# Two lag matrices at the end of the scan's program instead of among the late state products

## The chip, the cores and the metric

The kernel runs on one core of one Trainium2 chip. The metric is the device time of one execution in microseconds; the kernel before takes 1023.78 us (median of three runs, 1023.33 to 1025.45).

## The reference, cut to what matters

One layer of a diffusion backbone over 1024 latent tokens and 256 context tokens, of width 1024: a bidirectional state-space mixer (S5: 64 groups of 16 channels with 64 complex states each, a scan forward and one backward), a GELU and a gated linear unit, then a feed-forward block (SwiGLU, hidden width 2816), with adaptive norms around both.

```python
def s5_direction(u_ctx, u_lat, ...):
    lam_bar = exp(lam * exp(log_step))
    b_bar = ((lam_bar - 1) / lam) * b
    def run(u, h0):
        bu = einsum('lgh,gnh->lgn', u, b_bar);  bu[0] += lam_bar * h0
        h = associative_scan(h[l] = lam_bar * h[l-1] + bu[l])
        return einsum('lgn,ghn->lgh', h, c).real, h[-1]
    y_c, h_c = run(u_ctx, 0)
    y_l, _ = run(u_lat, h_c)
    return y_c, y_l
...
g = gelu(y_forward + y_backward + d_skip * h)
x = x + gate * (g * sigmoid(g @ w_glu + b_glu))
x = x + gate2 * swiglu(modulate(rms_norm(x)))
return rms_norm(x, norm_final)
```

## The kernel before, in words

The sequence is cut into 160 chunks of 8 tokens (32 of context, 128 of latents). Inside a chunk the outputs that come from the chunk's own inputs are a product with a lag matrix (a Toeplitz matrix made of c, the powers of lam_bar and b_bar, for each group); what comes from earlier chunks is a product of c times powers with the state at the chunk's start. The states themselves come from a serial scan over the chunks on VectorE (`scan()`, line 77 with LTa, LTb and ltc in PSUM), which runs while the other engines prepare what they can.

The 64 groups are held in four quarters of 16, and each quarter in two halves of 8; so there are eight halves, k = 0 to 7. Quarters 0 to 2 (k = 0 to 5) get their output in two steps: an early one that needs only the first half of the scan, and a late one for the second half of the latents. The last quarter (k = 6 and 7) gets all of it in one step at the end.

The order of the work around the change is written by hand as two strings of letters, PROG1 and PROG2; `run(prog)` goes through them and calls a function for each. Each engine works through its own instructions in that order. The scan's instructions are issued to VectorE ahead of both, so PROG1 is what the other engines do meanwhile. The letters that matter:

- C: the factors of c and powers of a quarter, on GpSimd (the last of them C33; the last quarter's lie in the region c3).
- K: `k_mats`, the lag matrices of one half. 144 small matmuls on TensorE (lines 809, 813 and 817; each with its weight load) write two PSUM banks, of which only some rows are written, so the banks are zeroed first. ScalarE copies each bank to SBUF (line 821) and issues a write of it to a table in HBM (line 822, tensor kd). K0 to K5 are in PROG1, zeroed by ScalarE (line 771) or standing in banks that keep their zeros (kt and pm). K6 and K7 are in PROG2; their banks are zeroed there by VectorE memsets (letters k6 and k7, line 966).
- T: `toeplitz`, SP reads a shifted quarter of a table back into SBUF (line 830). T12 to T15 belong to the last quarter.
- P and Y: the early product of a half (lines 945 and 922) and its two copies out of PSUM on ScalarE (line 997). P5 is the last.
- M2, m0, F30, F31: small products on GpSimd and a read by SP; F fills in the states between those that the scan has made, for the last quarter.
- Z, N, D, H: the late step of k: a turned copy of the states (Z, on VectorE or ScalarE, lines 902 and 904), the product (N, 64 matmuls, line 922), the addition on VectorE (D) and the GELU on ScalarE (H).
- Q: the whole product of a half of the last quarter (lines 945 and 935); it reads what T has brought.
- I and J: transposes of the activations for the GLU (line 1056) and their split in two parts for precise products; w and l: SP's reads of GLU weights (lines 1024 and 1048); W and V: the weights' split by VectorE, ScalarE and GpSimd; g: the first GLU products.

After PROG1 the PSUM pools of that stage are closed and eight banks (tile pe) opened in their place; a bank of the new pool is free when the last reader of the old one is done.

Of the kernel before, what the change touches and what calls it, by code (L numbers as in the profile page):

```python
# [25 lines left out]
HC = 16  # L26
# [2 lines left out]
MAGIC = 12582912.0  # L29
HOWS = "PPPP PPEE PEEE EEEE"  # L30
ZEN = "VVSVSVSV"
PROG1 = ("A22 B0 A26 C02 G1 A30 A34 C03 A40 K0 A44 A48 C10 K1 L2 A54 G2 C11 A60 F10 C12 F11 C13 T0 T1 T2 T3 A64 M0 M1 K2 R0 P0 Y0 Y1 K3 L3 R1 C20 P1 Y2 Y3 T4 T5 G3 T6 T7 C21 C22 C23 K4 R2 P2 Y4 Y5 K5 R3 P3 Y6 Y7 T8 T9 T10 T11 C30 C31 R4 P4 Y8 Y9 C32 C33 R5 P5 Y10 Y11 M2 m0 F30 F31")
PROG2 = ("k6 Z0 N0 Z1 Z2 D0 Z3 N1 k7 D1 Z4 H0 H1 K6 N2 D2 H2 K7 T12 T13 T14 T15 N3 Z5 D3 H3 N4 D4 z6 z7 I0 J0 I1 J1 w0 w1 l1 H4 N5 D5 I2 J2 H5 I3 J3 W0 W1 x0 x1 x2 x3"
         " Q6 H6 I4 J4 Q7 b0 I5 J5 H7 g03 g13 I6 J6 g23 g05 g15 I7 J7 V1 w20 w21 g26 x10 x11 x12 x13")
LOG2E = 1.4426950408889634
LN2H = 0.693359375
# [6 lines left out]
def s5_ffn_kernel(tc, a, out):  # L43
    nc = tc.nc
    V, S, E, PE, SY = nc.vector, nc.scalar, nc.gpsimd, nc.tensor, nc.sync
    ctx = ExitStack()
    with ctx:
        ctx.enter_context(tc.manual_schedule())
        sb = ctx.enter_context(tc.tile_pool(name="sb", bufs=1))
        def region(tag, kb, dt=F32):  # L50
            return sb.tile([P, int(kb * 256)], dt, tag=tag, name=tag)
# [12 lines left out]
        R0 = region("r0", 7)  # L64
# [79 lines left out]
        def pw(shape=(4, P)):  # L144
            return pW.tile([P] + list(shape), F32, tag="w", name="pw", bufs=NW[0])
# [613 lines left out]
        pm = pW.tile([P, 512], F32, tag="m", name="pm")  # L759
# [10 lines left out]
        def zeros(t):  # L770
            S.copy(t, cpk[:, 0:1].to_broadcast([P, 15 * HC]))
            return t

        kt = zeros(pA.tile([P, 15 * HC], F32, tag="r3", name="kt"))
# [24 lines left out]
        def bb(q, d, ri, a_):  # L799
            return BBn[q // 2][:, ri, d, 8 * (q % 2) + a_]  # L800

        def k_mats(q, hq, kts):

            tiles = [(g_, 2 * gi + hq, kts[g_][32 * gi:32 * gi + HC], slice(64 * g_, 64 * g_ + 64), (64 * g_, 32 * gi))
                     for gi in range(4) for g_ in range(2)]
            for d, c0, c1, ts_ in ((1, 128, 240, slice(7, 0, -1)), (0, 0, 112, slice(6, None, -1))):
                for ri in range(2):
                    for g_, a_, kv, ps, tp in tiles:
                        PE.matmul(kv[:, c0:c1], bb(q, d, ri, a_)[ps], CL[q][ps, ri, d, a_, ts_], start=ri == 0, stop=ri == 1,
                                  tile_position=tp)  # L810
            for g_, a_, kv, ps, tp in tiles:
                l0 = 64 * g_ + HC * (tp[1] // 32)
                PE.matmul(kv[:, 112:128], ident[ps, l0:l0 + HC], KD[ps, q, hq], start=True, stop=False, tile_position=tp)
            for d in range(2):
                for ri in range(2):
                    for g_, a_, kv, ps, tp in tiles:
                        PE.matmul(kv[:, 112:128], bb(q, d, ri, a_)[ps], Cs[q % 2][ps, 0, ri, d, a_], start=False,
                                  stop=d + ri == 2, tile_position=tp)
            for g_ in range(2):
                gq, kx = 2 * hq + g_, KX[2 * hq + g_]  # L820
                S.copy(kx, kts[g_])
                S.dma_start(KD_[q][:, gq], kx)
# [52 lines left out]
        def mod_cols(part):  # L875
            r8 = view(RA, 0, [4, P])
            if part == 0:
                S.copy(r8, pm.rearrange("p (j n) -> p j n", j=4))
                for i in range(2):
                    SY.dma_start(MBd[i], r8[96 * i:96 * i + 2].rearrange("p j n -> p (j n)"))  # L880
            elif part == 1:
                pt = pw()
                for j in range(4):
                    PE.transpose(pt[:, j], r8[:, j], ident)
                for h in range(2):
                    S.copy(mcol[:, :, 4 * h:4 * h + 4].rearrange("p b j -> p j b"), pt[:, :, h:P:32])
            elif part == 2:
                E.tensor_copy(mod2[:, 0], mcol[:, 1])
                tt(mod2[:, 1], mcol[:, 2], epsc[:, 1:2].to_broadcast([P, T]), ADD, E)
                tt(mod2[:, 1], mod2[:, 1], nrm[:, 1], MUL, E)  # L890
# [63 lines left out]
        def run(prog):  # L954


            for w in prog.split():
                op, i = w[0], int(w[1:])
                if op == "A":
                    ada(i)  # L960
                elif op == "M":
                    mod_cols(i)
                elif op == "k":
                    KT[i] = [pe8([15 * HC]) for _ in range(2)]
                    for kv in KT[i]:
                        V.memset(kv, 0.0)
                elif op == "K":
                    k_mats(*divmod(i, 2), KT.get(i) or [kt, zeros(pw([15 * HC])) if i < 4 else pm[:, 0:15 * HC]])
                elif op == "L":
                    cs_load(i, S)  # L970
                elif op == "G":
# [66 lines left out]
                elif op == "g":  # L1038
                    glu_mm(0, i // 10, range(i % 10 + 1))

        KT = {}
        late, W0, WR, PZ, GH, GR = {}, [], [], {}, [None, None], []
        wr0 = [view(RXa, 4, [1024]), view(RW, 0, [1024])]
        bglu = view(RU, 32, [D])
# [5 lines left out]
        def pe8(shape, tag="e", bufs=8):  # L1050
            return pE.tile([P] + list(shape), F32, tag=tag, name="pe", bufs=bufs)
# [51 lines left out]

        HOW = [[{"P": PE, "Y": SY, "E": E, "V": V}[c] for c in h] for h in HOWS.split()]
        run(PROG1)
        psW.__exit__(None, None, None)
        psA.__exit__(None, None, None)
        psE = tc.tile_pool(name="psE", bufs=1, space=bass.MemoryType.PSUM, reuse_waits="tile")
        pE = psE.__enter__()
        run(PROG2)  # L1110
        W0, GR = W0[0], GR[0]
        X1 = region("c3", 16)
# [92 lines left out]
        for cq in range(4):  # L1205
            for s in range(4):
                k = 4 * cq + s
# [61 lines left out]
        G2 = region("c3", 16, R32)  # L1269
# [420 lines left out]
        for i, (kind, ft, j) in enumerate(seq):  # L1690
# [12 lines left out]
            if kind == "U":  # L1703
# [4 lines left out]
                if (ft, j) in LAST:  # L1708
                    k, h = LAST[ft, j]
# [63 lines left out]
```

## Time and profile before

| | us |
|---|---|
| median of three runs | 1023.78 (1023.33 to 1025.45) |
| profiled execution, span | 1022.5 |
| TensorE busy | 962.6 (94%) |
| VectorE busy | 785.6 (77%) |
| GpSimd busy | 762.7 (75%) |
| ScalarE busy | 438.5 (43%) |

The profile gives the execution's own time only as its span, from the first instruction to the last; the runs' time is taken around it. In what follows a row of a timeline has the start, the duration, the engine, the line and the operation with the tiles that it writes and reads, and in brackets the idle time before it with what ended it. PEld is TensorE's weight load, which overlaps its matmuls; SPq and ACTq are transfers issued by SyncE and ScalarE. Tile names have no buffer numbers.

### The profile page before, as it was taken

The page shows a single profiled execution, that of the slowest core. Times are in us where ns is not written, and L with a number is a line of the kernel's source. Part 1 is how long each engine was busy: PE and PEld are TensorE (multiplying, and loading weights), DVE is VectorE, ACT ScalarE, POOL GpSimd, SP SyncE. Part 2 cuts the span into 40 slices and gives each one's busy share as a digit, 9 for nine tenths or more (in the row PEclk, how much of TensorE's full clock was granted, in tenths as well). Part 3 has the DMA queues.
Part 4 walks back from the last instruction along what each step waited for, and adds up shares of the span by engine and source line. Part 5 has one row for each costly group of instructions (what it writes and reads, how often), then busy time and mean ns, then how long its engine had stood idle before and what let it go on. Part 6 is the DMA issues. An engine that isn't in the chain of part 4 may idle for free. (4 is left out here: it accounts for less than half of the span.)

```text
span 1022.5 us, 18552 instructions
## 1 busy us (share of the span) xinstructions
PE 962.6 (94%) x6988; PEld 774.2 (76%) x6988; DVE 785.6 (77%) x1642; ACT 438.5 (43%) x858; POOL 762.7 (75%) x590
## 2 busy tenths in 40 slices
PE   5987798868999999999999999999999999999996
PEld 1466523658999988778888888888888888888885
DVE  7989799994365778788968768585958778686977
ACT  5477622324353663533334343424333343324337
POOL 5799999991591457879686877778686877777664
PEclk9999999998999999999999999999999999999998
DMA  9765997222622021011212011121212111121205
GB/s 318 292 132 96 276 350 243 91 73 57 235 80 86 2 104 62 21 42 42 83 41 73 32 52 61 43 73 52 73 42 81 41 40 56 45 70 52 72 21 165
DMA packets 48546, 98.96 MB, mean 97 GB/s; under 512 B 4284, under 2 KB 18876, under 8 KB 47176
## 3 DMA queue, kind: packets, MB, share of 16 engines
q1 hardware_dynamic: 43272, 86.64, 25.3%
q0 software_dynamic: 2016, 7.34, 3.8%
q10 hardware_dynamic: 3168, 3.79, 1.1%
q8 instruction: 55, 0.90, 0.4%
q14 instruction: 35, 0.29, 0.1%
HBM read 84.25 MB, written 6.17 MB: 88 GB/s over the span
## 5 line engine op out<-in xcount | busy, mean ns | idle before, releaser
L77 POOL TENSOR_TENSOR c<-rxc,c 128x512 fp32r<-128x512 f32 x128 | 166.6, 1316 | 53.5 <-ACT c L1227 52.7
L1287 PE MATMUL ut<-ra,c 128*128 128x512 f32 x400 | 155.7, 389 | 1.2 <-DVE ra L77 1.2
L1286 PE MATMUL ut<-ra,c 128*128 128x512 f32 x400 | 155.7, 389 | 0.2 <-ACT ra L1227 0.2
L1288 PE MATMUL ut<-ra,c 128*128 128x512 f32 x400 | 155.6, 389 | 0.0
L1227 ACT CAST c<-rxc 128x512 fp32r<-128x512 f32 x128 | 79.1, 622 | 146.8 <-PE xt L1581 53.3
L1581 PE MATMUL xt<-c,c 128*128 128x512 f32 x540 | 129.7, 389 | 0.0
L1581 PEld LDWEIGHTS xt<-c,c 128*128 128x128 f32 x540 | 101.4, 188 | 21.0
L77 DVE TENSOR_TENSOR ru<-ru,xt 128x1024 f32<-128x1024 f32 x90 | 106.8, 1213 | 8.6 <-PE xt L1581 6.6
L77 DVE TENSOR_TENSOR ru<-ut,ru 128x512 f32<-128x512 f32 x98 | 67.1, 686 | 43.1 <-PE ut L1288 37.7
L1287 PEld LDWEIGHTS ut<-ra,c 128*128 128x128 f32 x400 | 75.1, 188 | 17.1 <-POOL rxc L77 1.5
L1286 PEld LDWEIGHTS ut<-ra,c 128*128 128x128 f32 x400 | 75.1, 188 | 16.1 <-ACT ra L1227 0.6
L1288 PEld LDWEIGHTS ut<-ra,c 128*128 128x128 f32 x400 | 75.1, 188 | 15.5
L77 POOL TENSOR_TENSOR c<-rw,c 128x512 fp32r<-128x512 f32 (+1 forms) x29 | 42.5, 1465 | 38.8 <-ACT c L1227 38.2
L1286 PE MATMUL ut<-c,c 128*128 128x512 f32 x160 | 62.3, 389 | 0.8 <-DVE rxa L77 0.8
L77 POOL TENSOR_TENSOR c<-ru,c 128x512 fp32r<-128x512 f32 (+1 forms) x39 | 55.5, 1422 | 10.1 <-ACT c L1227 5.7
L77 POOL TENSOR_TENSOR rxc<-rxc 128x512 f32<-128x512 f32 x40 | 61.5, 1536 | 1.6
L1288 PE MATMUL ut<-c,c 128*128 128x512 f32 x160 | 62.3, 389 | 0.0
L1287 PE MATMUL ut<-c,c 128*128 128x512 f32 x160 | 62.3, 389 | 0.0
L1581 PE MATMUL ut<-c,c 128*128 128x512 f32 x216 | 51.9, 389 | 0.0
L584 PE MATMUL pv<-ru,c 128*64 128x160 f32 x512 | 43.7, 312 | 7.3 <-POOL ru L77 2.6
L77 DVE TENSOR_TENSOR pe<-pe,ru 128x256 f32<-128x256 f32 x64 | 27.4, 428 | 29.5 <-ACT pe L1127 17.4
L77 DVE TENSOR_TENSOR ru<-ru,ut 128x512 f32<-128x512 f32 x76 | 47.2, 678 | 0.7 <-ACT ru L1635 0.5
(449 smaller groups left out, 2576.0 us busy)
## 6 DMA issues: line engine op xcount, KB each, us to landing
c<-in_ada_w SPq DMA_DIRECT2D x46, 256.0 KB
rxc<-in_w SPq DMA_DIRECT2D x38, 256.0 KB
rxc<-in_w SPq DMA_DIRECT2D x19, 512.0 KB
ru<-in_w SPq DMA_DIRECT2D x11, 512.0 KB
rw<-in_w SPq DMA_DIRECT2D x11, 512.0 KB
ra<-in_ada_w SPq DMA_DIRECT2D x10, 512.0 KB
ra<-in_ada_w SPq DMA_DIRECT2D x18, 256.0 KB
ru<-in_xT SPq DMA_DIRECT2D x4, 1024.0 KB
```

Of the source, the lines that this page charges most:

```text
L77: eng.tensor_tensor(out=o, in0=x, in1=y, op=op)
L584: PE.matmul(pv[64 * (i % 2):64 * (i % 2) + 64, ri, c0:c0 + 160], w[:, i, 64 * ri:64 * ri + 64], U[:, 8 * b + 4 * j + i], start=True, stop= ...
L1227: S.copy(o[0], x)
L1286: PE.matmul(pu, wh, bh, start=start, stop=False)
L1287: PE.matmul(pu, wh, bl, start=False, stop=False)
L1288: PE.matmul(pu, wl, bh, start=False, stop=stop)
L1581: PE.matmul(pd, w[:, cs_], b, start=j in (1, 2, 4) and n == 0, stop=n == 2, skip_group_check=j not in (1, 2, 4))
```

## The change

K6 and K7 move from PROG2 to PROG1, behind the copies of the last early product (Y10, Y11) and ahead of M2, K7 first. K7 uses the banks kt and pm as K5 does, with no new zeros; K6 gets two banks of the pool pw, zeroed by ScalarE. The four VectorE memsets go. T12 to T15 stand first in PROG2 now, and the reads w0, w1 and l1 of the GLU weights stand after H2 and ahead of N3, no longer behind J1.

```diff
-PROG1 = ("... R5 P5 Y10 Y11 M2 m0 F30 F31")
-PROG2 = ("k6 Z0 N0 Z1 Z2 D0 Z3 N1 k7 D1 Z4 H0 H1 K6 N2 D2 H2 K7 T12 T13 T14 T15 N3 Z5 D3 H3 N4 D4 z6 z7 I0 J0 I1 J1 w0 w1 l1 H4 N5 D5 I2 J2 H5 I3 J3 W0 W1 x0 x1 x2 x3"
+PROG1 = ("... R5 P5 Y10 Y11 K7 K6 M2 m0 F30 F31")
+PROG2 = ("T12 T13 T14 T15 Z0 N0 Z1 Z2 D0 Z3 N1 D1 Z4 H0 H1 N2 D2 H2 w0 w1 l1 N3 Z5 D3 H3 N4 D4 z6 z7 I0 J0 I1 J1 H4 N5 D5 I2 J2 H5 I3 J3 W0 W1 x0 x1 x2 x3"
          " Q6 H6 I4 J4 Q7 b0 I5 J5 H7 g03 g13 I6 J6 g23 g05 g15 I7 J7 V1 w20 w21 g26 x10 x11 x12 x13")
...
-                elif op == "k":
-                    KT[i] = [pe8([15 * HC]) for _ in range(2)]
-                    for kv in KT[i]:
-                        V.memset(kv, 0.0)
                 elif op == "K":
-                    k_mats(*divmod(i, 2), KT.get(i) or [kt, zeros(pw([15 * HC])) if i < 4 else pm[:, 0:15 * HC]])
+                    k_mats(*divmod(i, 2), [zeros(pw([15 * HC])) if i == 6 else kt, zeros(pw([15 * HC])) if i in (0, 1, 2, 3, 6) else pm[:, 0:15 * HC]])
```

TensorE's order at the end of the early products and through the late ones, as a piece of the difference (pw are PROG1's banks, pe those of PROG2; the rows of K7, which alternate between kt and pm, stand just ahead of this piece):

```order
+L809 MATMUL pw<-c_66,rxa 16x112 x32
+L813 MATMUL pw<-r_60 16x16 x8
+L817 MATMUL pw<-rxc,rxa 16x16 x32
 L922 MATMUL pe<-c_63,ra 64x128 x64
-L809 MATMUL pe<-c_66,rxa 16x112 x32
-L813 MATMUL pe<-r_60 16x16 x8
-L817 MATMUL pe<-rxc,rxa 16x16 x32
-L922 MATMUL pe<-c_64,ra 64x128 x32
-L809 MATMUL pe<-c_66,rxa 16x112 x32
-L813 MATMUL pe<-r_60 16x16 x8
-L817 MATMUL pe<-rxc,rxa 16x16 x32
-L922 MATMUL pe<-c_64,ra 64x128 x32
```

K6 now stands ahead of the late products N0 and N1 (the row of 64), and nothing stands between N1, N2 and the later ones.

ScalarE's order behind Y11, as a piece of the difference:

```order
+L821 COPY rw<-kt 128x240
+L822 DMA kd_1249<-rw 128x240
+L821 COPY rw<-pm 128x240
+L822 DMA kd_1249<-rw 128x240
+L771 COPY pw<-r_60 128x240 x2
+L821 COPY r_60<-pw 128x240
+L822 DMA kd_1249<-r_60 128x240
+L821 COPY r_60<-pw 128x240
+L822 DMA kd_1249<-r_60 128x240
 L902 COPY ra<-ra 128x512 x2
-L1006 ACT_TABLE_LOAD
-L1006 ACTIVATE ru<-ru 128x1024 x2
```

K7's two copies and writes, the two zero copies for K6, and K6's copies and writes now come ahead of the turned copies Z2 and Z4 (line 902) and of the first GELU; before, they stood behind the first two GELUs.

TensorE's rows at the start of N0 with the change, with the engines that each waits for:

```order
L817 MATMUL pw<-rxc,rxa 16x16 x32
L922 MATMUL pe<-c_63,ra 64x128 [waits DVE_49,PE_49]
L922 MATMUL pe<-c_63,ra 64x128 [waits Activation_49]
L922 MATMUL pe<-c_63,ra 64x128 [waits DVE_49]
L922 MATMUL pe<-c_63,ra 64x128 x29
L922 MATMUL pe<-c_63,ra 64x128 [waits Activation_49]
```

The second row's wait for ScalarE is for the copy of K6's first bank, which N0 now writes; the third row waits for the turned copy Z0 on VectorE. The last row is N1's start: it waits for the copy of K6's second bank. Before, N0's banks were those of P5, and K6's banks were its own.

More of the change, by code (lines that the diff above doesn't have):

```diff
@@ L31 @@
 ZEN = "VVSVSVSV"
-PROG1 = ("A22 B0 A26 C02 G1 A30 A34 C03 A40 K0 A44 A48 C10 K1 L2 A54 G2 C11 A60 F10 C12 F11 C13 T0 T1 T2 T3 A64 M0 M1 K2 R0 P0 Y0 Y1 K3 L3 R1 C20 P1 Y2 Y3 T4 T5 G3 T6 T7 C21 C22 C23 K4 R2 P2 Y4 Y5 K5 R3 P3 Y6 Y7 T8 T9 T10 T11 C30 C31 R4 P4 Y8 Y9 C32 C33 R5 P5 Y10 Y11 M2 m0 F30 F31")
-PROG2 = ("k6 Z0 N0 Z1 Z2 D0 Z3 N1 k7 D1 Z4 H0 H1 K6 N2 D2 H2 K7 T12 T13 T14 T15 N3 Z5 D3 H3 N4 D4 z6 z7 I0 J0 I1 J1 w0 w1 l1 H4 N5 D5 I2 J2 H5 I3 J3 W0 W1 x0 x1 x2 x3"
+PROG1 = ("A22 B0 A26 C02 G1 A30 A34 C03 A40 K0 A44 A48 C10 K1 L2 A54 G2 C11 A60 F10 C12 F11 C13 T0 T1 T2 T3 A64 M0 M1 K2 R0 P0 Y0 Y1 K3 L3 R1 C20 P1 Y2 Y3 T4 T5 G3 T6 T7 C21 C22 C23 K4 R2 P2 Y4 Y5 K5 R3 P3 Y6 Y7 T8 T9 T10 T11 C30 C31 R4 P4 Y8 Y9 C32 C33 R5 P5 Y10 Y11 K7 K6 M2 m0 F30 F31")
+PROG2 = ("T12 T13 T14 T15 Z0 N0 Z1 Z2 D0 Z3 N1 D1 Z4 H0 H1 N2 D2 H2 w0 w1 l1 N3 Z5 D3 H3 N4 D4 z6 z7 I0 J0 I1 J1 H4 N5 D5 I2 J2 H5 I3 J3 W0 W1 x0 x1 x2 x3"
          " Q6 H6 I4 J4 Q7 b0 I5 J5 H7 g03 g13 I6 J6 g23 g05 g15 I7 J7 V1 w20 w21 g26 x10 x11 x12 x13")
@@ L1039, in run @@
                     glu_mm(0, i // 10, range(i % 10 + 1))
-        KT = {}
         late, W0, WR, PZ, GH, GR = {}, [], [], {}, [None, None], []
```

## The prediction, as put on record

> **What bounds the kernel now.** I read the busy times by stretch first, then the timelines of TensorE, VectorE and ScalarE around the end of the scan, then who waited for whom. Times are of the profiled execution (span 1022.5 us; the median of the runs is 1.28 us more, which I take as what lies around the span).
>
> Busy time of each engine by stretch (window, length, PE, PEld, DVE, ACT, POOL, granted clock, DMA):
>
> ```profile
> 267.50:300.00 32.50, 32.50 (x278) 32.50 (x276) 16.08 (x35) 19.25 (x41) 28.25 (x16) 1.00 0.33 115
> 300.00:330.00 30.00, 30.00 (x252) 30.00 (x252) 16.22 (x47) 11.66 (x40) 7.43 (x5) 1.00 0.33 106
> 330.00:985.00 655.00, 652.61 (x3043) 546.15 (x3041) 500.53 (x660) 264.94 (x489) 499.48 (x371) 1.00 0.16 53
> ```
>
> From 267.5 us, where the GLU products begin, to 985 us TensorE idles 2.4 us in all. What brings TensorE to the GLU sooner moves the end by as much, if its operands come along. So the question is the stretch before it. TensorE's timeline there (start, duration, engine, line; the idle time before it and its releaser in brackets):
>
> ```profile
> 221.75 2.26 PE L922 MATMUL pw<-c,ra 64*64 64x128 f32 x64
> ...
> 228.72 0.70 PE L922 MATMUL pe<-c,ra 64*64 64x128 f32 x4 [4.71 <-DVE ra L77]
> 229.77 6.44 PE L922 MATMUL pe<-c,ra 64*64 64x128 f32 x124 [0.35 <-DVE ra L904]
> ...
> 253.17 1.06 PE L945 MATMUL pe<-ra,ru 128*128 128x128 f32 x8
> ...
> 254.71 1.16 PE L945 MATMUL pe<-ra,ru 128*128 128x128 f32 x8 [0.48 <-DMA ra<-kd]
> ```
>
> The scan's program ends on TensorE at 224.01 (221.75 + 2.26). Then TensorE idles 4.71 us for the scan itself, and the first late product, N0, gets going at 229.77. The scan runs on VectorE:
>
> ```profile
> 228.28 0.29 DVE L77 TENSOR_TENSOR ra<-ltc,ra 128x128 f32<-128x128 f32 x1
> 228.62 0.52 DVE L966 MEMSET pe<- 128x240 f32 x2
> 229.05 1.54 DVE L904 COPY ra<-ra 128x512 f32<-128x512 f32 x2
> ```
>
> Its last addition ends at 228.57; two memsets for the first lag matrix and the copy Z0 follow, and N0 waits for that copy. From 229.77 to Q6, the first product of the last quarter (253.17), TensorE is the queue that the others wait for. There the two lag matrices stand in its way (weight loads, one for each matmul):
>
> ```profile
> 236.13 0.80 PEld L809 LDWEIGHTS pe<-c,rxa 64*16 64x16 f32 x64
> 236.84 0.28 PEld L813 LDWEIGHTS pe<-r 64*16 64x16 f32 x16
> 237.03 0.68 PEld L817 LDWEIGHTS pe<-rxc,rxa 64*16 64x16 f32 x64
> 237.74 1.57 PEld L922 LDWEIGHTS pe<-c,ra 64*64 64x64 f32 x46
> 240.13 0.81 PEld L922 LDWEIGHTS pe<-c,ra 64*64 64x64 f32 x18 [0.81 <-issue]
> 241.06 0.79 PEld L809 LDWEIGHTS pe<-c,rxa 64*16 64x16 f32 x64
> 241.76 0.28 PEld L813 LDWEIGHTS pe<-r 64*16 64x16 f32 x16
> 241.95 0.40 PEld L817 LDWEIGHTS pe<-rxc,rxa 64*16 64x16 f32 x30
> 243.58 0.31 PEld L817 LDWEIGHTS pe<-rxc,rxa 64*16 64x16 f32 x34 [1.23 <-issue]
> 243.92 3.08 PEld L922 LDWEIGHTS pe<-c,ra 64*64 64x64 f32 x94
> 247.58 1.31 PEld L922 LDWEIGHTS pe<-c,ra 64*64 64x64 f32 x34 [0.59 <-issue]
> ```
>
> K6 is 144 matmuls from 236.13 to 237.74 (1.61 us), K7 144 more from 241.06 to 243.92 (2.86 us, with a stop inside). The list of waits has the three stops on the matmul side:
>
> ```profile
> PE pe L817 <- issue: 1.1, 1, 1.1
> PE pe L922 <- issue: 1.0, 2, 0.6
> ```
>
> They stand in a fixed rhythm: from 240.13 to 243.58 there are 18 + 64 + 16 + 30 = 128 pairs of load and matmul, and from there to 247.58 34 + 94 = 128 again, so 256 instructions each time, in 3.45 and 4.00 us. A block of 256 seems not to be had faster than that. 128 pairs of the state products take some 4.5 us (2 x 2.26) and hide it; the quick K matmuls do not. So the stops belong to K6 and K7, and move with them.
>
> **The change part by part.**
>
> *Removed between N1 and Q6.* 253.17 - 236.13 = 17.04 us stand there now. Less K6 1.61, less K7 2.86 (its 1.1 us stop included), less the other two stops 1.0: 11.57 us are left. The 0.48 us that Q6 waits for its table goes too: the four table reads would start some 14 us earlier (below), Q6 only 5. They now take from 247.96 to about 254.71, where that wait ends:
>
> ```profile
> 247.96 4.39 SPq L830 DMA_DIRECT2D ra<-kd  x4
> ```
>
> *K7 in the idle time.* Its bank is free since the copies of K5 (before 207), and its last factor comes from GpSimd, where C33 ends at 222.49:
>
> ```profile
> 220.12 2.37 POOL L77 TENSOR_TENSOR c<-c,rw 128x1024 f32<-128x1024 f32 x1
> ```
>
> So K7 starts at 224.05 and needs 1.6 us. But counting pairs back from the stop at 240.13 (46 of N2, 144 of K6, 128 of N0 and N1 are 636 instructions), a block border lies about 131 instructions before the end of the last early product, at 221.7; the next falls on K7's 125th instruction, at 224.8, and by 3.45 to 4.0 us a block it is not ready before 225.2 to 225.7. K7 ends at 226.1 to 226.7.
>
> *ScalarE between K7 and K6.* Two bank copies and two table writes, then two new zero copies, stand in its queue before K6 may start. The same for K5, a zero copy of K2, and a slow table write:
>
> ```profile
> 175.31 0.39 ACT L771 COPY pw<-r 128x240 f32<-128x240 f32 x1
> ...
> 186.61 1.63 ACTq L822 DMA_DIRECT2D kd<-rw  x1
> ...
> 205.49 0.36 ACT L821 COPY rw<-kt 128x240 f32<-128x240 f32 x1 [0.57 <-PE pm L817]
> ...
> 207.01 0.62 ACT L902 COPY c<-ra 128x512 f32<-128x512 f32 x1 [0.40 <-ACT rw L821]
> ```
>
> 1.52 us (207.01 - 205.49) and 2 x 0.37: K6 starts at 228.4 to 229.0, and 1.61 us later, with 0 to 0.2 for its block, ends at 230.0 to 230.8. Of K7 and its 4.71 us of cover little is left over: this is the term that costs.
>
> *N0.* It waits for ScalarE's copy of K6's first bank, which is now its own (0.36 and the signal: 0.45). It starts at 230.5 to 231.2, against 229.77 before. The scan's copies, without the four memsets, are done by then (228.57 + 1.54 = 230.1): VectorE no longer decides. The ScalarE copies that N2 needs come after K6's two copies, about 232.5, in time for N2. The block border falls on N0's 30th matmul, reached at 231.9 to 232.6 and ready at 232.3 to 233.7.
>
> *The clock.* The granted clock goes in windows of 3.41 us (columns as above):
>
> ```profile
> 194.28:197.69 3.41, 0.95 (x86) 0.93 (x85) 3.41 (x21) 1.51 (x3) 3.25 (x2) 1.00 0.57 173
> 197.69:201.10 3.41, 3.41 (x76) 3.37 (x69) 3.38 (x21) 1.33 (x3) 3.33 (x3) 0.50 0.32 100
> 207.93:211.34 3.41, 2.00 (x60) 1.81 (x56) 3.20 (x15) 1.38 (x3) 3.41 (x2) 1.00 0.25 71
> 211.34:214.76 3.42, 1.34 (x9) 1.18 (x10) 3.18 (x14) 0.21 (x1) 3.34 (x3) 1.00 0.59 149
> 214.76:218.17 3.41, 3.41 (x40) 3.19 (x43) 3.17 (x14) 0.00 (x0) 3.41 (x3) 0.50 0.31 95
> 228.41:231.82 3.41, 2.75 (x44) 2.39 (x48) 2.12 (x5) 2.42 (x3) 3.33 (x5) 0.50 0.00 0
> 231.82:235.24 3.42, 3.42 (x72) 3.42 (x68) 1.70 (x4) 0.42 (x1) 2.97 (x5) 0.50 0.02 5
> 235.24:238.65 3.41, 3.41 (x200) 3.25 (x196) 1.77 (x4) 1.73 (x3) 0.00 (x0) 1.00 0.02 5
> ```
>
> A window with 0.95 or 1.34 us of TensorE work is followed by one at 0.50; one with 2.00 is not; a full one brings 1.00 back, one with 2.75 did not. So N0 and N1 ran at half clock until 235.24, 3.42 / 72 = 48 ns a matmul; at full clock it is 2.26 / 64 = 35 ns. With the change, 225.0 to 228.4 holds about 1 us of K7: half clock again is likelier than not. What that does to K6 has one near row, K4's last matmuls, part of which fell into the half-clock window at 197.69, together with K5's (minimum, median and maximum in ns):
>
> ```profile
> L817 PE MATMUL pm<-rxc,rxa x64: 172/183/202, 197.5 to 205.3; 64*16 64x16 f32 x64
> ```
>
> At most 202 ns instead of 172, and they overlap: I charge K6 nothing. The bounds are nothing and a doubling, 1.6 us. So the 98 matmuls after N0's 30th take 3.4 us at full clock, 4.7 at half: N1 ends at 235.7 to 238.4, say 236.8. That is no earlier than the 236.13 of before.
>
> The Trainium skill, "TensorE: Matmul & The Clock Gate", Part 1 (the HAM clock gate), puts the drop after one or more idle windows of about 3.4 us. With K6 and K7 in the gap no window would be idle, and TensorE would stay at full clock (the first rival below); the rows of 0.95 and 1.34 us speak against so strict a reading.
>
> The skill's "Runtime: NRT & Kernel Launch", Instruction fetch mechanics, also has the instructions come in blocks of 256 and calls a border mostly hidden. If it were so for the K matmuls, the sum would lose the late blocks before K6 and in N0, about a microsecond. The three stops say otherwise here.
>
> *Sum.* Q6 starts at 236.8 + 11.57 = 248.4 (247.3 to 250.0) instead of 253.17: 4.8 us; with the table wait 5.2 (3.7 to 6.4). I take 5.1 off, since the earlier table and weight reads may cost a block a few tenths: 1023.78 - 5.1 = **1018.7 us**.
>
> *What comes along.* The GLU weights' reads stand behind the table reads on SP, and these hang on K6's table write (about 232.4, and by my estimate 2 us to land). So both start some 14 us earlier, once GpSimd's fills, which do not move, have freed one of the buffers. The weights' splitting then waits for nothing but TensorE's own products. The tightest follower is the second quarter's split:
>
> ```profile
> 276.86 4.61 POOL L77 TENSOR_TENSOR ra<-rxc,ra 128x2048 fp32r<-128x2048 f32 x1 [4.25 <-ACT ra L1073]
> ```
>
> It ends at 281.47, when TensorE needs it (281.6), but it starts after a ScalarE cast that itself follows TensorE's transposes, so it keeps its distance.
>
> **Rivals.**
>
> *The clock stays up and no block is late.* N0 from 230.5, 128 x 35 ns: N1 ends at 235.0, Q6 at 246.6, a gain of 6.6 + 0.5: 1016.7. For it: the windows' grid may lie otherwise in other executions, and the gap is only 2.3 us. Against: the 1.34 us row. 14%.
>
> *The ScalarE chain is longer.* One table write at 1.63 instead of 0.33 us (186.61) makes K6 1.3 us later; with half clock throughout, the gain is 3.7 - 1.3 = 2.4: 1021.4. 17%.
>
> *A follower is pinned.* If the second quarter's split kept its 281.47, through GpSimd or a late weight read, TensorE would wait there and all would be lost: 1023.8. Against: each of its predecessors follows TensorE. 8%.
>
> *Slower.* N0 is queued behind K6, and K6 behind ScalarE's table writes. If one of those waited for an earlier transfer to land, as long as the table reads take (254.71 - 247.96 = 6.75 us), N0 would start at 237.6 and the gain of 5.1 turn into a loss of 1.7: 1025.5. It decides from 5.1 us of lateness. Against: the slowest of these rows is 1.63 us. 5%.
>
> That the order does not change is excluded by the rows shown with the change.
>
> **How the numbers follow.** Forecast 56%, the rivals 14, 17, 8 and 5. The forecast's own range is 1017.4 to 1020.1; with the first two rivals, 1016.6 to 1021.4. A measurement of this kernel tells about 0.2% (2 us) from nothing: faster by that 0.84 (the first three, less 3 for the edge of the second), same 0.11, slower 0.05.
>
> **What would show it.** K7 within 224 to 227 on TensorE, K6 starting between 228.4 and 229.0 after ScalarE's zero copies; N0 at 230.5 to 231.2 and released by ScalarE, no longer by VectorE; Q6 between 247.3 and 250.0 without a wait for its table; no other idle time up to 985. It is wrong if N0 starts later than 232, if stops by issue add up to more than 2 us after N0, or if TensorE waits anew between 255 and 300.

## The result, and the profile after

The changed kernel takes 1017.59 us (median of 20 runs, 1015.05 to 1023.01), the kernel before beside it 1022.5 us (20 runs, 1021.02 to 1025.45): a ratio of 0.9953, 95% interval 0.9941 to 0.9965, so 4.9 us faster. The forecast was 1018.7, its range 1016.6 to 1021.4; it took 5.1 us off the 1023.78 that three runs had given, which twenty put at 1022.5.

The profiled execution took 1015.21 us (span 1013.4), 2.4 below the median of its kernel; that of before, with the same 1.8 us around its span of 1022.5, took some 1024.3, about 1.8 above the median beside it. The two traces are 9.1 us apart, nearly twice the medians' difference; so what the pair shows is compared below with further traces.

Busy time by stretch from the GLU's start on, of the change (window, length, PE, PEld, DVE, ACT, POOL, granted clock, DMA):

```profile
258.79:975.00 716.21, 713.80 (x3563) 607.80 (x3562) 529.47 (x739) 295.06 (x567) 529.06 (x385) 1.00 0.18 58
```

and the same stretch of the kernel before:

```profile
267.49:985.00 717.51, 715.12 (x3569) 608.66 (x3566) 532.83 (x741) 295.85 (x568) 535.17 (x390) 1.00 0.18 58
```

TensorE idles 2.4 us in both. From the GLU's start (258.79) to the end of the span it is 754.6 us with the change, 755.0 before. So what lies behind the GLU's start took nothing back and gave 0.4 us at most; the rest of this text looks at what lies ahead of it. TensorE's timeline there, with the change:

```profile
221.38 2.28 PE L922 MATMUL pw<-c,ra 64*64 64x128 f32 x64
...
227.31 1.24 PE L809 MATMUL pw<-c,rxa 64*16 64x112 f32 x59 [2.04 <-ACT pw L771]
...
228.52 0.75 PE L817 MATMUL pw<-rxc,rxa 64*16 64x16 f32 x62
229.58 0.69 PE L922 MATMUL pe<-c,ra 64*64 64x128 f32 x4 [0.31 <-DVE ra L77]
230.62 10.57 PE L922 MATMUL pe<-c,ra 64*64 64x128 f32 x316 [0.35 <-DVE ra L904]
...
245.27 1.39 PE L945 MATMUL pe<-ra,ru 128*128 128x128 f32 x11
247.00 0.72 PE L945 MATMUL pe<-ra,ru 128*128 128x128 f32 x5 [0.34 <-issue]
```

P5 ends at 223.66, K7 follows (to 225.27), TensorE waits 2.04 us for ScalarE's zero copies, K6 runs from 227.31 to 229.27, and N0 goes on from 230.62 (its first four matmuls wait for the scan alone, the fifth for the copy Z0). From there 316 matmuls run without a stop at 33 ns each; before, the first 124 of them took 6.44 us (52 ns each), and K6, K7 and three stops stood among the others. Q6 starts at 245.27 instead of 253.17, and no row waits for the tables. ScalarE between K7 and N2:

```profile
225.33 0.36 ACT L821 COPY rw<-kt 128x240 f32<-128x240 f32 x1 [0.57 <-PE pm L817]
...
226.90 0.65 ACT L771 COPY pw<-r 128x240 f32<-128x240 f32 x2 [0.40 <-ACT rw L821]
229.37 0.36 ACT L821 COPY r<-pw 128x240 f32<-128x240 f32 x1 [1.82 <-issue]
...
230.88 1.14 ACT L902 COPY ra<-ra 128x512 f32<-128x512 f32 x2 [0.40 <-DVE ra L904]
```

The first zero copy stands 1.57 us behind the first bank copy (226.90 - 225.33), as K5's row had it (1.52). Of the two that N0 waits for, the copy of K6's first bank ended at 229.73 (229.37 + 0.36); the scan's last addition ended at 229.43 in this execution, late, and its copy Z0 was the last to come. SP's reads:

```profile
232.30 4.07 SPq L830 DMA_DIRECT2D ra<-kd  x4
236.42 1.81 SPq L1020 DMA_DIRECT2D rxa<-in_w_glu  x1
```

They start 15.7 and 16.0 us earlier than before.

### The profile page after: what moved, and what is told of

Read it like the earlier page. It is cut to its first block, busy times and chain, and to the rows that moved or that the text cites. A ratio compares the mean times of both kernels' runs of the same rounds, so it can differ in the third digit from the quotient of the medians.

```text
span 1013.4 us, 18560 instructions
## 1 busy us (share of the span) xinstructions
PE 959.4 (95%) x6988; PEld 772.1 (76%) x6988; DVE 780.4 (77%) x1638; ACT 438.9 (43%) x860; POOL 763.4 (75%) x590
```

## The experiments

They ran in three groups. The kernel before stood at 1022.85 us (11 runs) beside the first four, at 1023.09 (17 runs) beside the next four and at 1023.05 (29 other runs, on another chip) beside the last four; ratios are against those. Each fp32 product of this kernel stands as two matmuls in the timelines: a call in the order pieces ahead is two of the matmuls counted here.

### The change once more

No edit; a second trace, and times beside the variants.

> The changed kernel once more, nothing altered, for a second trace and more times. The one trace there is has Q6 15.7 us behind the scan's last addition (24.6 before) with full clock from N0 on and no stop by issue; its execution (1015.2 us) was 2.4 us below the median of its kind. If the clock's windows make that difference, this trace has half clock or stops behind N0 wherever its execution is nearer to the median of 1017.6, with Q6 17 to 20 us behind the scan's end. If K6 and K7 off the path are all of it, Q6 stands 15.5 to 16.5 us behind the scan's end whatever the execution's time. Median against the kernel before 0.9945 to 0.996 by both.

Measured: 1016.17 us (6 runs), ratio 0.9938 (0.9926 to 0.9949). TensorE, a row of its weight loads and, below them, the clock's windows:

```profile
227.92 1.82 PE L809 MATMUL pw<-c,rxa 64*16 64x112 f32 x57 [2.23 <-ACT pw L771]
...
230.56 9.72 PE L922 MATMUL pe<-c,ra 64*64 64x128 f32 x285
240.58 0.64 PE L922 MATMUL pe<-c,ra 64*64 64x128 f32 x12 [0.30 <-issue]
...
231.12 8.97 PEld L922 LDWEIGHTS pe<-c,ra 64*64 64x64 f32 x283 [0.27 <-ACT r L821]
```

```profile
224.66:228.07 3.41, 1.18 (x113) 1.03 (x97) 3.20 (x14) 1.81 (x6) 3.33 (x6) 1.00 0.15 48
228.07:231.48 3.41, 3.41 (x154) 2.93 (x156) 1.98 (x6) 0.46 (x3) 3.33 (x5) 0.50 0.10 33
```

Here the window ahead of K6 held 1.18 us of work, the next was granted half the clock, and K6 took 2.71 us (227.92 to 230.63) instead of 1.96. The scan (228.80) was done by then; N0's first matmuls followed K6 directly, and its loads then waited for ScalarE's copy of K6's first bank until 231.12. In the first trace the windows had held more, and none fell:

```profile
223.07:226.48 3.41, 2.20 (x162) 1.97 (x158) 3.17 (x14) 1.77 (x4) 3.25 (x8) 1.00 0.19 61
226.48:229.90 3.42, 2.28 (x147) 2.02 (x148) 3.12 (x13) 1.03 (x4) 3.34 (x6) 1.00 0.23 77
```

From the scan's end to the GLU's start it is 29.36 us in the first trace and 30.62 in this one (38.92 before). Q6 stands 17.36 us behind the scan's end (246.16 - 228.80), 15.84 in the first trace: the distance is not fixed. As I read the rows, half clock in K6 is a part of that; the other is that the scan ended earlier here, so that N0 waited for K6 and ScalarE. The ratio lies just below the 0.9945 to 0.996 of both expectations.

### The matrices moved, the reads left in their places

The change, but the reads stand in PROG2 as before:

```diff
-PROG2 = ("T12 T13 T14 T15 Z0 N0 ... D2 H2 w0 w1 l1 N3 ... I1 J1 H4 ..."
+PROG2 = ("Z0 N0 ... D2 H2 T12 T13 T14 T15 N3 ... I1 J1 w0 w1 l1 H4 ..."
```

> K7 and K6 in PROG1 as in the change, but the four table reads and the three reads of GLU weights at their old places among the late products. If TensorE's freed time is the gain (my reckoning), it is the whole gain less 0 to 0.5 us for the table wait of Q6: 4.3 to 5.1 us below before. If the earlier reads are part of it (rival), half of the gain or less is left: 1 to 2.5 us, and TensorE waits for the tables or the weights' split between Q6 and the first GLU product.

Measured: 1017.27 us, ratio 0.9944 (0.9932 to 0.9956), the change within the noise. SP's rows:

```profile
234.49 4.43 SPq L830 DMA_DIRECT2D ra<-kd  x4
238.97 2.02 SPq L1020 DMA_DIRECT2D rxa<-in_w_glu  x1
```

K6 ended 2.2 us later in this execution (231.48), and so do the reads start; relative to K6 they start at the same time as in the change. What starts them is K6's tables, not their place among the letters. TensorE's order is the change's here, and the clock did what the prediction had let it do:

```profile
226.78:230.19 3.41, 1.37 (x106) 1.08 (x98) 3.05 (x10) 1.37 (x4) 3.33 (x5) 1.00 0.24 77
230.19:233.60 3.41, 3.41 (x139) 3.06 (x122) 0.00 (x0) 1.23 (x3) 3.33 (x6) 0.50 0.15 44
```

Half clock fell on the end of K6 and on N0, and the 320 matmuls from N0 on took 11.76 us, 37 ns each instead of 33.

### K7 alone

Only K7 moves; K6 stays behind H1 with its memsets.

```diff
-PROG1 = ("... Y10 Y11 M2 m0 F30 F31")
-PROG2 = ("k6 Z0 N0 ... N1 k7 D1 Z4 H0 H1 K6 N2 D2 H2 K7 T12 ..."
+PROG1 = ("... Y10 Y11 K7 M2 m0 F30 F31")
+PROG2 = ("k6 Z0 N0 ... N1 D1 Z4 H0 H1 K6 N2 D2 H2 T12 ..."
```

> K7 alone moved to PROG1, K6 left among the late products with its memsets, the reads at their old places. My reckoning: K7 lay on the path with 2.86 us (1.1 of it a stop), and no zero copies or bank copies hold N0 now, so 2.5 to 4 us below before. If the clock's state behind the gap is the gain (rival), K7 alone, 1.6 us of work in a gap of 4.7, changes it little: 0.5 to 2 us.

Measured: 1018.85 us, ratio 0.9952 (0.9940 to 0.9964): 4.0 us faster than before, 2.7 slower than the change beside it.

```profile
227.79 0.70 PE L922 MATMUL pe<-c,ra 64*64 64x128 f32 x4 [3.46 <-DVE ra L77]
228.85 6.46 PE L922 MATMUL pe<-c,ra 64*64 64x128 f32 x124 [0.36 <-DVE ra L904]
236.85 1.26 PE L922 MATMUL pe<-c,ra 64*64 64x128 f32 x30
239.07 5.45 PE L922 MATMUL pe<-c,ra 64*64 64x128 f32 x162 [0.96 <-issue]
```

N0 keeps its old start (scan's end + 1.2 us) and its half clock (6.46 us for 124), and one stop is left where before there were three. So K7 brings its own time and two stops. K6 brings the other 2.7 us: its own 1.6 us and the last stop go, and N0 is no longer wholly at half clock, but in its new place K6 pushes N0 back (its fifth matmul comes 1.2 us behind the scan's end in the change's first trace and 2.3 in the second). How these share the 2.7 us was not measured apart.

### Zeros first

ScalarE zeroes K6's banks ahead of K7's copies, so that K6 needs nothing behind K7:

```diff
-PROG1 = ("... Y10 Y11 K7 K6 M2 m0 F30 F31")
+PROG1 = ("... Y10 Y11 O6 K7 K6 M2 m0 F30 F31")
...
+                elif op == "O":
+                    ZB.extend(zeros(pw([15 * HC])) for _ in range(2))
...
+                    k_mats(*divmod(i, 2), ZB if i == 6 else [...])
```

> The change, but K6's two banks are zeroed before K7's copies, so that K6 follows K7 on TensorE without waiting for ScalarE. My reckoning, which has N0 held by ScalarE's chain by 0.6 to 1.4 us: 0.5 to 1.5 us below the changed kernel. If N0 waits for the scan anyway, as the one trace of the changed kernel has it (rival): the same as the changed kernel within 0.5 us, or slower by up to 1.5 us, since K6 and K7 back to back leave a longer idle stretch ahead of N0 and outrun their instruction blocks.

Measured: 1015.46 us, ratio 0.9931 (0.9913 to 0.9949); the change's interval is 0.9926 to 0.9949, so no difference can be told.

```profile
225.26 1.03 PE L809 MATMUL pw<-c,rxa 64*16 64x112 f32 x45
228.12 0.46 PE L809 MATMUL pw<-c,rxa 64*16 64x112 f32 x18 [1.84 <-issue]
...
229.24 1.74 PE L922 MATMUL pe<-c,ra 64*64 64x128 f32 x29
231.96 4.39 PE L922 MATMUL pe<-c,ra 64*64 64x128 f32 x130 [0.99 <-issue]
```

K6 starts at 225.26, right behind K7, and then stops: 1.84 us in K6, 0.99 after N0's 29th matmul, 128 matmuls further on. The wait for ScalarE is gone, and stops that the profile puts down to no engine, in the rhythm of 256 instructions, have taken its place. I read them as waits for code; the shifted kernel below bears on that.

### TensorE kept busy ahead of K6, with eight products

The change with idle work between K7 and K6 (four calls; each gives two matmuls of 0.43 us):

```diff
-PROG1 = ("... Y10 Y11 K7 K6 M2 m0 F30 F31")
+PROG1 = ("... Y10 Y11 K7 X4 K6 M2 m0 F30 F31")
...
+                elif op == "X":
+                    d = pw([512])
+                    for n in range(i):
+                        PE.matmul(d, ident, RC[2][:, 0:512], start=True, stop=True)
```

> The change, with four products whose results nobody uses (128x512, fp32, into one of the scan stage's banks) between K7 and K6, in the 2.0 to 2.2 us in which TensorE waits for the zero copies. Question: does the half clock that sometimes follows this gap cost anything in the changed kernel? In the change's first trace no window at half clock fell here, and the time from the scan's end to the GLU's start was 29.36 us; in its second one the window from 228 us on was at half clock, K6 took 2.71 us instead of 1.7 to 2.0, and that time was 30.62. Clock theory: TensorE is busy from 224 on, no window after 224 falls to half, K6 takes 1.6 to 2.0 us, the time from the scan's end to the GLU's start is 29.0 to 30.0, and the median is 0 to 1 us below the change's. Rival (the dummy products are only in the way; K6 starts late, at 228.5 or later, since they need longer than the gap): that time 30.5 or more, and no gain or a loss of up to 1 us. Rival (block stops come back, as when K6's zeros stood first, since the gap in which blocks are loaded is filled): stops by issue of 1 to 2 us in K6 or N0 and no gain.

Measured: 1017.95 us, ratio 0.9950 (0.9932 to 0.9967). I had counted four matmuls; there were eight, 3.4 us in all, and K6 started at 229.55, more than a microsecond late. No window fell to half clock after 220, but N0 stopped for 1.24 us and Q6 for 1.19. There was too much idle work, so the run tells of the clock only that keeping it up did not pay for this.

### The same ahead of N0 in the kernel before, with eighteen

```diff
-PROG1 = ("... Y10 Y11 M2 m0 F30 F31")
+PROG1 = ("... Y10 Y11 X9 M2 m0 F30 F31")
```

with the letter X of above.

> The kernel before, with nine products whose results nobody uses (128x512, fp32) in the 4.7 us in which TensorE waits for the scan's end; nothing moved. It measures by itself what the half clock after that gap cost in the kernel before, and so how much of the change's gain is the clock and how much is the place of K6 and K7. Clock theory: N0 and N1 take 35 ns a matmul instead of 48, K6 starts at scan end + 6 instead of + 7.6 us, and the time is 1.0 to 1.7 us below the kernel before. Place theory (the gain is K6 and K7 themselves, with their stops, and N0 and N1 at half clock cost little since the stops make up for it): below 0.5 us. In both, K6, K7 and the three stops stay between N1 and Q6, so nothing near the change's 5 to 6 us.

Measured: 1024.80 us, ratio 1.0018 (1.0006 to 1.0031), slower, for the same miscount:

```profile
224.74 7.99 PE L972 MATMUL pw<-c,r 128*128 128x512 f32 x18
...
233.57 4.24 PE L922 MATMUL pe<-c,ra 64*64 64x128 f32 x124 [0.41 <-DVE ra L904]
```

N0 is some 4 us late, and the kernel loses only 1.7: N0 and N1 took 4.24 us instead of 6.44.

### The same with eight

```diff
-PROG1 = ("... Y10 Y11 M2 m0 F30 F31")
+PROG1 = ("... Y10 Y11 X4 M2 m0 F30 F31")
```

> The kernel before, with eight products whose results nobody uses (128x512, fp32, 0.43 us each by the run with eighteen of them, 3.4 us in all) in the idle time ahead of N0, now so few that N0 is not held up: they end about 227.5 to 228, the scan at 227.5 to 229.5. It measures the half clock after the gap in the kernel before by itself. Clock theory: N0 and N1 at 33 to 35 ns a matmul (4.2 us for 124) instead of 6.4 us; from N0's effective start to the GLU's start 34.6 us, as in the run with eighteen, instead of 37.7; 2 to 3 us faster than the kernel before. Rival (half clock costs nothing that the stops by issue do not give back): below 0.7 us.

Measured: 1021.05 us, ratio 0.9984 (0.9972 to 0.9995): 1.6 us faster than before by the ratio (0.5 to 2.9), with not one product of use moved.

```profile
229.68 4.24 PE L922 MATMUL pe<-c,ra 64*64 64x128 f32 x124 [0.41 <-DVE ra L904]
...
238.09 1.25 PE L922 MATMUL pe<-c,ra 64*64 64x128 f32 x26 [1.11 <-issue]
242.09 0.51 PE L817 MATMUL pe<-rxc,rxa 64*16 64x16 f32 x42 [1.49 <-issue]
```

N0 starts on time and gains 2.2 us; the stops, now 1.11 and 1.49 instead of 0.62, 1.13 and 0.40, take back 0.45. In the kernel with only the reads moved (the last one below), whose order on TensorE is that of before, the same 124 took 5.12 us, so the full 2.2 us are not lost in every execution. Half clock in N0 and N1 cost the kernel before something between the two expectations, and what TensorE gains in quick small products is in part handed to the arrival of code.

### K6 and K7 where TensorE idles anyway

Both stand behind K5, computed from the third quarter's factors, since the last quarter's do not exist yet; so the last quarter's lag matrices, and all that comes of them, are other numbers.

```diff
-PROG1 = ("... Y4 Y5 K5 R3 P3 ... Y10 Y11 K7 K6 M2 m0 F30 F31")
+PROG1 = ("... Y4 Y5 K5 K7 K6 R3 P3 ... Y10 Y11 M2 m0 F30 F31")
...
+                    k_mats(min(i // 2, 2), i % 2, [...], i // 2)
```

> The change, with K6 and K7 put behind K5, where TensorE idles anyway (210 to 215 us), so that neither stands between the early products and N0. Their factors are not made yet there, so they are computed from the third quarter's factors instead: the last quarter's lag matrices, and what is computed from them, are not the reference's, while each instruction has its shape and place in the tables. It measures what K6 and K7 still cost in the changed kernel. Theory (they cost about what N0 starts later: the scan's last copy Z0 decides N0 instead of K6's first bank copy, 0.8 to 2 us earlier, but then N0 and N1 run behind a gap of 4.7 us at half clock, 1.6 us more): the time from the scan's end to the GLU's start is 29 to 30 us, and the median within 1 us of the change's. Rival (the ScalarE chain behind K7 is what the change still pays, 2 us or more): 27 to 28 us, and 1.5 to 2.5 us faster than the change.

Measured: 1013.97 us, ratio 0.9912 (0.9893 to 0.9931): 9.0 us below the kernel before. Against the change's two ratios it is 2.7 to 4.2 us lower, more than both expectations.

```profile
225.30 2.28 PE L923 MATMUL pw<-c,ra 64*64 64x128 f32 x64
228.71 5.66 PE L923 MATMUL pe<-c,ra 64*64 64x128 f32 x157 [1.13 <-DVE ra L77]
235.00 5.47 PE L923 MATMUL pe<-c,ra 64*64 64x128 f32 x163 [0.64 <-issue]
```

P5 ends here at 227.58, nearly 4 us later than with the change, and it costs nothing: the scan, at 228.65, still comes after it. N0 follows the scan directly, and the GLU starts at 257.58. In the change's second trace, 0.25 us from the median beside it, the scan ends alike (228.80), but N0 starts at 230.56 and the GLU at 259.42: 1.8 us later, all of it in N0's start. The time from the scan's end to the GLU's start, 28.93 us, is near the theory's, though without the half clock that the theory had there (none was granted after 214.1); the gain is nearer the rival's. So the change still pays for having K7, ScalarE's copies and K6 between P5 and N0: 1.8 us in these two traces, 2.7 to 4.2 by the ratios.

### The kernel before with half a block of code more

```diff
-PROG1 = ("... Y10 Y11 M2 m0 F30 F31")
+PROG1 = ("... Y10 Y11 X32 M2 m0 F30 F31")
...
+                        PE.matmul(d[0:16, 0:16], ident[0:64, 0:16], RC[2][0:64, 0:16], start=True, stop=True)
```

> The kernel before, with 32 products whose results nobody uses (64x16x16, fp32; 64 pairs of weight load and matmul, 128 instructions, about 0.7 us) in TensorE's 4.7 us of idle time ahead of N0. Block theory (the stops by issue stand every 256 instructions of TensorE, wherever that falls): the three stops, which stood after 46 matmuls of N2's first half, after 30 of K7's last 64 and after 94 of the next product, each come 64 matmuls earlier: inside K6 or at its end, in K7's first 64 or at their end, and after 30 of the next product; the time stays within 1 us. Rival (the stops belong to the operations, for example to the change of operand from one kind of product to the next): they stay where they were.

Measured in a single run, so its time is not compared: 1020.57 us.

```profile
236.23 0.27 PE L817 MATMUL pe<-rxc,rxa 64*16 64x16 f32 x18 [0.48 <-issue]
...
239.96 0.46 PE L809 MATMUL pe<-c,rxa 64*16 64x112 f32 x17 [0.49 <-issue]
...
243.41 3.49 PE L922 MATMUL pe<-c,ra 64*64 64x128 f32 x98 [1.08 <-issue]
```

The stops stood after 46 matmuls of N2, after 30 of K7's 64 in line 817 and after 94 of N3 and N4. Now they stand with 18 matmuls of K6 left, with 18 of K7's 64 in line 809 left (one of them is shown on its own), and after 30 of N3: each 64 pairs earlier in the program. They belong to the count of instructions, not to the operation. The page of the kernel before has transfers that fit such a block: TensorE's matmuls and as many loads on the first line below, the queue of instructions on the second (transfers, MB):

```profile
PE 962.6 (94%) x6988; PEld 774.2 (76%) x6988; DVE 785.6 (77%) x1642; ACT 438.5 (43%) x858; POOL 762.7 (75%) x590
...
q8 instruction: 55, 0.90, 0.4%
```

2 x 6988 instructions by 256 are 54.6, and there are 55 transfers of 0.90 MB / 55 = 16.4 KB.

### The change with four products ahead of K6, and with half a block

The first has two calls of the large product, the second 32 of the small one, both between K7 and K6:

```diff
-PROG1 = ("... Y10 Y11 K7 K6 M2 m0 F30 F31")
+PROG1 = ("... Y10 Y11 K7 X2 K6 M2 m0 F30 F31")
...
+PROG1 = ("... Y10 Y11 K7 X32 K6 M2 m0 F30 F31")
```

> The change, with four products whose results nobody uses (128x512, fp32, 1.7 us in all, four instructions and their weight loads) between K7 and K6, half of what held K6 up before: they end at about 227.4 to 227.8, when the zero copies end. Clock theory: no window at half clock after 224, K6 1.7 to 2.0 us; blocks of code keep their rhythm, since eight instructions move a border by a thirty-second of a block; from the scan's end to the GLU's start 29.3 to 30.5 us, median 0.5 to 1.5 us below the change's (1016.2 and 1017.6 in two sets of runs). Rival (the change's executions differ by the scan's end alone, not by the clock): no change of the median.

> The change, with 32 products whose results nobody uses (64x16x16, fp32; 64 pairs of weight load and matmul, 128 instructions, half a block, 1.76 us by the run of them in the kernel before) between K7 and K6. They fill the same idle time as the four larger products of the kernel beside it, but bring half a block of code more. Block theory (the stretch from K7 to the end of N1 in the changed kernel goes as fast as blocks of 256 instructions arrive, 3.4 to 4 us each, the idle time ahead of K6 included): the stops come back, by half a block in all, so N1 ends 1 to 1.8 us later and the GLU starts as much later than in the kernel beside it; median 0.5 to 1.8 us above that one's. Rival (blocks are no limit in the changed kernel, since no stop by issue is to be seen there): the same time as the kernel beside it.

Measured: 1016.38 us, ratio 0.9939 (0.9921 to 0.9957), for the four; 1019.56 us, 0.9964 (0.9953 to 0.9975), for the half block. The traces, of the slowest of six and of twelve runs. The first:

```profile
229.53 1.24 PE L809 MATMUL pw<-c,rxa 64*16 64x112 f32 x59 [0.32 <-ACT pw L771]
...
233.77 6.49 PE L922 MATMUL pe<-c,ra 64*64 64x128 f32 x205 [1.27 <-issue]
...
243.97 1.51 PE L922 MATMUL pe<-c,ra 64*64 64x128 f32 x39 [1.98 <-issue]
```

The second:

```profile
230.90 0.57 PE L968 MATMUL pw<-c,r 64*16 64x16 f32 x17 [1.57 <-issue]
...
234.54 0.45 PE L817 MATMUL pw<-rxc,rxa 64*16 64x16 f32 x35 [1.81 <-issue]
```

With the four, no window fell after 220, and the median is the change's: a steady clock here brought nothing that can be seen. The interval (1.8 us to either side) leaves room for a part of the clock theory's 0.5 to 1.5 us, and the two stops of 1.27 and 1.98 us in this trace may have taken it back. With half a block more in the same idle time, two stops of 3.4 us in all stand ahead of N0, and the kernel is 2.6 us slower by the ratios (1019.56 against 1016.38 by the medians). Two stops came back ahead of N0, 127 matmuls apart, so blocks are a limit in the changed kernel. The 2.6 us are more than the half block's 0.5 to 1.8, and the stops are not all of it:

```profile
232.26:235.67 3.41, 1.60 (x106) 1.47 (x91) 0.00 (x0) 0.36 (x1) 1.69 (x3) 0.50 0.00 0
235.67:239.08 3.41, 3.41 (x72) 3.41 (x68) 0.41 (x1) 1.82 (x4) 0.00 (x0) 0.50 0.26 79
```

Two windows at half clock lie on the end of K6 and on N0 and N1 (72 matmuls in 3.41 us, 47 ns each). What part of the 2.6 us is the clock's and what the stops' is not shown.

### The weight reads alone

The kernel before, with w0, w1 and l1 right behind T15:

```diff
-PROG2 = ("... K7 T12 T13 T14 T15 N3 ... J0 I1 J1 w0 w1 l1 H4 ..."
+PROG2 = ("... K7 T12 T13 T14 T15 w0 w1 l1 N3 ... J0 I1 J1 H4 ..."
```

> The kernel before, with the reads of the first GLU weights (w0, w1, l1) moved ahead of N3, right behind T15; K6 and K7 stay. It takes the change's second part by itself. Theory: nothing between Q6 and the end waits for these weights, so 0, within 0.5 us. Rival (the splits of the weights wait for them and set when the first GLU products start, so part of the change's gain is theirs): 0.5 to 2 us faster. Rival (the earlier reads take the table reads' bandwidth): Q6 waits more than the 0.48 us of before, and up to 1 us slower.

Measured: 1022.54 us, ratio 0.9995 (0.9985 to 1.0006): nothing. Q6's wait stays too:

```profile
253.04 1.16 PE L945 MATMUL pe<-ra,ru 128*128 128x128 f32 x8 [0.43 <-DMA ra<-kd]
```

## Why the prediction was right, step by step

**What bounds it: right.** In all fourteen traces the time from the GLU's start to the end of the span is 754.6 to 755.1 us. Earlier reads brought nothing (0.9995), and no follower was pinned.

**The order of events: right.** K7 directly behind P5; ScalarE's chain between K7 and K6 (K6 2.04 and 2.23 us after K7's end, against 2.3 in the working); N0's fifth matmul at 230.62 and 231.14 (230.5 to 231.2 forecast). K6 itself started at 227.31 and 227.92, about a microsecond ahead of the 228.4 to 229.0 named as a sign, since K7 had no stop. N0 was released by ScalarE's side in the second trace, but by Z0 in the first, where the scan ended late. The table wait is gone.

**The late block: the rhythm was right, its place in the changed kernel wrong.** The 256 instructions held (the shifted kernel, the count of transfers), and where nothing else waits the stop falls on N0's 30th matmul, as counted (zeros first: after the 29th). But I charged 0.4 to 1.1 us for it there and 0.4 to 0.9 for K7, and neither is in the change's two traces. For N0 the reason is the 2 us that TensorE waits for ScalarE ahead of K6, which give the blocks the time to arrive: I had added up two waits that cover each other. The zeros-first kernel shows it from the other side. For K7 no such wait stands ahead. There the working had the border before it at 221.7; counted back pair by pair in the trace of before it lies at 221.32, 0.4 us earlier, and in the change's traces K7's border comes 3.4 us behind it (220.84 to 224.27 in the first) and N0's 3.3 and 3.1 us behind K6's, without a stop. So 3.45 us is no floor. The Trainium skill's sentence that borders are mostly hidden ("Runtime: NRT & Kernel Launch", Instruction fetch mechanics) agrees with the change's traces (0.3 us) and not with the zeros-first one (1.84 and 0.99).

**The clock: the place was off.** I let half clock begin at 228.4 and charged N0 and N1 for it and K6 nothing. In the second trace it fell on K6 (2.71 us instead of 1.96, and 1.6 forecast), in the first on nothing; N0 and N1 ran at 33 to 34 ns, some 4.3 us instead of the forecast's 6.0. So Q6 came at 245.27 and 246.16, earlier than the forecast's 247.3 to 250.0: this is the step that failed in these two traces. In the trace with the reads left, half clock did fall on N0, and Q6 came at 247.26. Where it falls changes from one execution to the next. The Trainium skill ("TensorE: Matmul & The Clock Gate", Part 1) puts the drop after an idle window; the window of 1.18 us of work that fell in the second trace does not agree with so strict a reading.

**The sum: close, in part by luck.** Beside the kernel before, the change gained 4.9 us in the first set of runs and 6.7 in the second, against 5.1 forecast (the two intervals of the ratio overlap, so a difference between the sets is not shown). In level the forecast is 1.1 us too high, since its base was 1.28 us above the median of before. But the terms are not those of the working: the late blocks did not come, half clock cost less in the two traces, and yet the gains stay 2.2 and 0.4 us under the 7.1 us of the rival without both, so losses that the working did not have stood in their place. That these came out about equal is luck. In the first trace the rival with a steady clock and no late block (1016.7) is what happened, with Q6 at 245.27 where it had 246.6. The medians of the change's two sets lie 0.9 us above and 0.5 below that rival, 1.1 and 2.5 below the forecast. One term that the working did not have, and that can make its executions differ (1015 to 1023 us), is P5. I had K7 start at 224.05, as a fixed number. By execution it differs, with the half-clock windows among the early products. From the traces (us):

| | half clock, 195 to 222 | P5 ends | scan ends | N0's fifth matmul | GLU starts |
|---|---|---|---|---|---|
| the change, first | 3.4 | 223.66 | 229.43 | 230.62 | 258.79 |
| the change, second | 3.4 + 3.4 | 224.08 | 228.80 | 231.14 | 259.42 |
| zeros first | 3.4 + 3.4 | 223.76 | 227.48 | 229.78 | 258.79 |
| reads left | 6.8 + 6.8 | 225.60 | 228.64 | 232.00 | 260.77 |
| four products | 6.8 + 6.8 | 225.69 | 228.39 | 231.64 | 262.86 |
| eight products | 3.4 + 6.8 | 224.38 | 228.08 | 231.39 | 261.60 |
| half a block | 3.4 + 6.8 | 226.60 | 227.72 | 235.20 | 264.46 |
| K6, K7 behind K5 | 3.4 + 3.4 | 227.58 | 228.65 | 229.27 | 257.58 |

(In the rows with products or half a block, N0 and the GLU also wait for these and for the stops shown above.) Before, P5 ended 4.6 us ahead of the scan and its delays cost nothing. With the change the chain is P5, K7, ScalarE, K6, N0: in the first five rows N0's fifth matmul comes 5.9 to 7.1 us behind P5, and no longer at the scan's end + 1.2. Only in the first trace did the scan come last. What a longer half-clock window does to P5 is seen in the windows of the kernel with four products:

```profile
209.59:213.00 3.41, 1.29 (x40) 1.10 (x32) 3.20 (x14) 1.59 (x3) 3.41 (x2) 1.00 0.37 85
213.00:216.42 3.42, 2.34 (x9) 2.15 (x10) 3.21 (x15) 0.00 (x0) 3.34 (x3) 0.50 0.61 131
216.42:219.83 3.41, 3.41 (x41) 3.19 (x43) 3.17 (x14) 0.00 (x0) 3.40 (x2) 0.50 0.41 98
```

P5 ends 1.5 to 2.0 us later where both stretches of half clock are 6.8 us long; with one of 3.4 and one of 6.8 it ended at 224.38 and at 226.60, so their length alone does not fix it. Where neither P5 nor ScalarE's chain can matter (K6 and K7 behind K5) the kernel is 2.7 to 4.2 us below the change. That P5's lateness is what separates the change's executions is read from these rows, not shown by a run that sets the clock among the early products; none was made. The trace with the reads left, P5 at 225.60, is of a run of 1017.29 us.

**The rivals.** The longer ScalarE chain did not come (the table writes took 0.33 us to issue, one 0.51), nor a pinned follower, nor the slower case.

## What to carry to other kernels

Work moved into an engine's waiting time is free only while its own predecessor is early: before moving it, ask how late that predecessor is in the slowest execution, since the move can turn its hidden delays into delays of the end. Waits that follow one another on one engine are not to be added where they can run at the same time (here code arriving while ScalarE zeroes a bank): removing one only shows the other. And a trace is one execution: where medians and traces differ by as much as the gain, take two traces of the same kernel before explaining the difference.

## What the hardware showed that I had not expected

Over the windows of 3.41 us from 16 to 1005 us in the fourteen traces, what the clock does next follows how much of a window TensorE was busy: of 43 windows at full clock with at most 1.44 us of work, every one was followed by half clock; of 28 with 1.45 to 1.91 us, 8; of 43 with 1.92 to 2.2 us, 5; above that one more was, with 2.79 us. At half clock all windows with 2.83 us or less kept it there, and all with 3.02 or more ended it (of three between, with 2.87, 3.01 and 3.01, two did). So a partly idle window is enough, and a few tenths of work on one side of a border or the other can decide 3.4 us at half speed; the amount of work does not settle every case.

Stops for code also appear far from small products. In the kernel with four products the one of 1.98 us at 243.97 stands among state products that had covered their blocks elsewhere, while the table and weight reads kept the DMA engines busy (a share of 0.91 from 240.31 to 243.72). In the change's own traces the like is 0.3 us. Whether the reads delay the code there was not tested.
